# Turning three of the four branch outputs through DRAM and VectorE instead of TensorE, in a two-layer hybrid mixer

## The chip, the cores and the metric

The program runs on one core of a Trainium2 chip. The metric is the device time of one execution in microseconds. Besides the matrix engine (TensorE, PE in the profile) the core has a vector engine (DVE), a scalar engine (ACT), GpSimd (POOL, which here does hardly anything but issue DMAs) and SyncE (SP, which issues the loads of the weights).

## The reference

The reference is a decoder trunk of two layers over 256 tokens of width 2048. Cut to what is computed in a layer:

```python
xn = rmsnorm(h)
z  = xn @ w_in                      # one projection, cut into segments
o0 = forgetting_attention(q, k, v, f) * silu(gate)      # "fox"
o1 = differential_attention(q, k, v)  * silu(gate)      # "diff"
o2 = rmsnorm(ssd_chunked(conv(xbc), dt) * silu(z))      # "ssd", Mamba-2
o3 = glu(gelu(s5_scan(u))) * silu(gate)                 # "s5"
# each o_n: 256 tokens x 512
m  = sum(sigmoid(g[n]) * (o[n] @ w_branch[n]) for n in range(4))
h  = h + rmsnorm(m @ w_out)
```

All is in float32. Every `o[n] @ w_branch[n]` needs `o[n]` with its 512 channels on the partitions, since TensorE contracts over partitions, while the branches leave it with the tokens on the partitions. So each of the eight blocks of 128 tokens by 512 channels in a layer (four branches, two token blocks) has to be turned. The change is to six of them.

## The kernel before, in words

The matrix products run as one long stream on TensorE. `plan()` (L48) lists the weight matrices in order, in column groups of 512; `group` (L404) does one group: for each k-tile of 128 rows of weights and each of the two token blocks three matmuls of 128 by 512, because the float32 operands are split in a high and a low part: high weight by high activation (L423), high by low (L424), low by high (L425). The weights come in chunks of four k-tiles by one SP DMA each of 1 MB (`prefetch`, L340) into `raw`. ACT makes the high part `wh` from it, and VectorE the low part `wl` as `raw - wh`, both two k-tiles at a time (128 by 1024 elements). There are five such half-chunk buffers of each kind. L101 and L113 are helpers for two-operand VectorE work and for ACT work, and L110 is VectorE's `scalar_tensor_tensor`, so many different things show those lines and are told apart by their tiles.

Everything else (attention, the convolution, the scans) is written as Python generators, which `pump` (L379) advances between chunks, as far as a budget of costs goes. A generator that yields WAIT pauses until the next chunk. `drain` (L397) runs a generator to its end. After that a scheduler fixes the order of the instructions on each engine, and each engine works its own list in order.

The branches `fox` (L462), `diff` (L551) and `ssd` (L640) leave their outputs in tiles `fxo`, `dfo` and `xst` (two each, one for each token block) in `st["o", n, tb]`. The gates of the merge follow in `plan()` as groups mg(n, cg) of 16 k-tiles, and after the four gate groups of a branch come its four products br(n, cg) of 4 k-tiles each. In the third chunk of mg(n, 0) the hook `turn_o` drains the branch and calls `o_split` (L531): for each token block four transposes on TensorE (`split_T`, L293, the instruction at L298) through a PSUM bank `mx`, then ACT copies the high part `oh` and VectorE makes the low part `ol`. The br groups use `oh` and `ol` as stationary operands. For the fourth branch the same is done late in its gates.

The S5 branch (`s5`, L779) runs beside the gates. For each of four slices of its channels it loads a table `s5b` (L838), writes `uu` to DRAM and fetches it back in another layout (`du` L852, `s5u` L862: four fetches of 128 KB), multiplies that with `s5bs` on TensorE (L885) and scans on VectorE. All of these DMAs stand on POOL's queue, which works its list in order; a DMA that has to wait for data holds up those behind it.

A second way of turning a block is in the kernel already, for q, k and the convolution's inputs: `put` (L315) writes a block to DRAM in four pieces, `get` (L321) reads it back with four neighbouring tokens on one partition (`shuf`), and VectorE's transpose of 32 by 32 blocks (`flip_pair`, L327) finishes it. The channels then come out in another order, given by the permutation P in `_layout` (L1213), and the columns of the weights that made them are permuted to match when the inputs are laid out on the host.

Of the kernel before, what the change touches and what calls it, by code (L numbers as in the profile page):

```python
# [10 lines left out]
F32 = mybir.dt.float32  # L11
# [6 lines left out]
ADD, SUB, MUL, MAX, MIN = ALU.add, ALU.subtract, ALU.mult, ALU.max, ALU.min  # L18
# [11 lines left out]
WAIT = -1  # L30
# [39 lines left out]
def trunk(ctx: ExitStack, tc: tile.TileContext, x, xT0, wall, cst, prm, rows, lam, normg, postg, s5b, s5c, out):  # L70
# [391 lines left out]
    def fox(st):  # L462
        lf = st["sp"]
        qT = [blk("foxqT", (128, 2, 256)) for _ in range(2)]
        kT = [blk("foxkT", (128, 2, 256)) for _ in range(2)]
        Xs = [[get(d) for d in st[src]] for src in ("fq", "fk")]
        yield WAIT
        yield WAIT
        for dst, X in zip((qT, kT), Xs):
            for hp in range(2):  # L470
                flip_pair(dst[hp], X, hp)
                yield 1.25
        bm = [blk("bm", (128, 3, 128)) for _ in range(4)]
        for kb in range(2):
            ps = mx()
            for hd in range(4):
                o = ps[:, hd * 128:(hd + 1) * 128]
                PE.matmul(o, lhsT=bc(lf[:, 0, hd:hd + 1], [128, 128]), rhs=bc(one, [128, 128]) if kb else U,
                          start=True, stop=kb == 0)
                if kb:  # L480
                    PE.matmul(o, lhsT=bc(lf[:, 1, hd:hd + 1], [128, 128]), rhs=U, start=False, stop=True)
            p3 = ps.rearrange("p (h k) -> p h k", h=4)

            for hd in range(4):
                tt(bm[hd][:, 2 * kb], p3[:, hd], tri, ADD)
                if kb == 0:
                    act(bm[hd][:, 1], p3[:, hd])
            yield 0.8
        yield WAIT
        E, pt, pso = {}, {}, {}  # L490
        rs = [small([128, 4], "fx_rs") for _ in range(2)]

        def scores(i):
            qb, hd = divmod(i, 4)
            nk = (qb + 1) * 128
            ps = mx()[:, 0:nk]
            PE.matmul(ps, lhsT=qT[hd // 2][:, hd % 2, qb * 128:(qb + 1) * 128], rhs=kT[hd // 2][:, hd % 2, 0:nk],
                      start=True, stop=True)
            S = blk("S", (128, 256))
            m = small([128, 1], "fx_m", bufs=4)  # L500
            b = bm[hd][:, 0] if qb == 0 else bm[hd][:, 1:3].rearrange("p a k -> p (a k)")
            V.tensor_tensor_reduce(out=S[:, 0:nk], in0=ps, in1=b, scale=1.0, scalar=-3.0e38,
                                   op0=ADD, op1=MAX, accum_out=m)
            ts(m, m, -1.0)
            E[i] = blk("E", (128, 256))
            act(E[i][:, 0:nk], S[:, 0:nk], AF.Exp, bias=m, scale=1.0, accum_out=rs[qb][:, hd:hd + 1])
            return 0.3 + 0.13 * qb

        def turn(i):
            pt[i] = probs_T(E.pop(i), i // 4 + 1)  # L510
            return 0.0

        def values(i):
            qb, hd = divmod(i, 4)
            if hd == 0:
                pso[qb] = mx()
            pv(pso[qb], pt.pop(i), st["fv"], hd, qb + 1)
            if hd < 3:
                return 0.0
            ri = small([128, 4], "fx_ri")  # L520
            V.reciprocal(ri, rs[qb])
            o = blk("fxo")
            for hd in range(4):
                c = slice(hd * 128, (hd + 1) * 128)
                stt(o[:, c], pso[qb][:, c], ri[:, hd:hd + 1], st["fg"][qb][:, c], MUL, MUL)
            st["o", 0, qb] = o
            return 1.0

        yield from pipeline(8, (scores, turn, values), STEP)

    def o_split(st, n):  # L531
        st["oT", n] = []
        for tb in range(2):
            oh, ol = blk("oh", (128, 4, 128), F32R), blk("ol", (128, 4, 128), F32R)
            split_T(lambda i: (oh, ol), st["o", n, tb], 4)
            st["oT", n].append((oh, ol))

    def rope(src, tb):
# [12 lines left out]
    def diff(st):  # L551
        l = st["l"]

        qT = [[blk("difqT", (128, 2, 256)) for _ in range(2)] for _ in range(2)]
        kT = [blk("difkT", (128, 2, 256)) for _ in range(2)]
        halves = [cs[:, C_HALF + a:C_HALF + a + 1] for a in range(2)]
        li = 0.8 - 0.6 * math.exp(-0.3 * l)
        sub = rw[:, l, R_SUB:R_SUB + 128].unsqueeze(1).to_broadcast([128, 4, 128])
        r = {}
        for nm in ("dq", "dk"):  # L560
            for tb in range(2):
                r[nm, tb] = rope(st[nm][tb], tb)
                yield 2.0
            g3 = st["dg"][nm == "dk"].rearrange("p (h d) -> p h d", h=4)
            tt(g3, g3, sub, MUL)
            yield 0.6
        yield WAIT
        Xs = {nm: [get(r[nm, tb]) for tb in range(2)] for nm in ("dk", "dq")}
        yield WAIT
        yield WAIT  # L570
        yield WAIT
        for hp in range(2):
            flip_pair(kT[hp], Xs["dk"], hp)
            yield 1.25
        for hp in range(2):
            full = blk("difqf", (128, 2, 256))
            flip_pair(full, Xs["dq"], hp)
            for a in range(2):
                act(qT[hp][a], full, AF.Copy, scale=halves[a])
            yield 1.25  # L580
        yield WAIT
        E, pt, pso, rs = {}, {}, {}, {}

        def scores(i):
            qb, hd = divmod(i, 4)
            nk = (qb + 1) * 128
            ps = mx().rearrange("p (a k) -> p a k", a=2)
            S = blk("S2", (128, 2, 256))
            E[i] = blk("E2", (128, 2, 256))
            m = small([128, 2], "df_m", bufs=4)  # L590
            rs[i] = small([128, 2], "df_rs", bufs=6)
            for a in range(2):
                PE.matmul(ps[:, a, 0:nk], lhsT=qT[hd // 2][a][:, hd % 2, qb * 128:(qb + 1) * 128],  # L593
                          rhs=kT[hd // 2][:, hd % 2, 0:nk], start=True, stop=True)
                V.tensor_tensor_reduce(out=S[:, a, 0:nk], in0=ps[:, a, 0:nk], in1=tri if qb == 0 else mask2,
                                       scale=1.0, scalar=-3.0e38, op0=ADD, op1=MAX, accum_out=m[:, a:a + 1])
            ts(m, m, -0.125)
            for a in range(2):
                act(E[i][:, a, 0:nk], S[:, a, 0:nk], AF.Exp, bias=m[:, a:a + 1], scale=0.125,
                    accum_out=rs[i][:, a:a + 1])  # L600
            return 0.5 + 0.26 * qb

        def combine(i):
            nk = (i // 4 + 1) * 128
            e, q = E[i], rs[i]
            V.reciprocal(q, q)
            tt(q[:, 1:2], q[:, 1:2], nlam[:, l], MUL)
            ts(e[:, 0, 0:nk], e[:, 0, 0:nk], q[:, 0:1])
            stt(e[:, 0, 0:nk], e[:, 1, 0:nk], q[:, 1:2], e[:, 0, 0:nk], MUL, ADD)
            return 0.5 + 0.2 * (i // 4)  # L610

        def turn(i):
            pt[i] = probs_T(E.pop(i)[:, 0], i // 4 + 1)
            return 0.0

        def values(i):
            qb, hd = divmod(i, 4)
            if hd == 0:
                pso[qb] = mx()
            pv(pso[qb], pt.pop(i), st["dv"], hd, qb + 1)  # L620
            if hd < 3:
                return 0.0
            o, sq = blk("dfo"), blk("dfsq")
            sq3 = sq.rearrange("p (h d) -> p h d", h=4)
            ss = small([128, 4], "df_ss")
            act(o, pso[qb])
            tt(sq, o, o, MUL)
            V.tensor_reduce(out=ss, in_=sq3, axis=AX.X, op=ADD)
            rst = small([128, 4], "df_rst")
            rsqrt(rst, ss, 4, 1.0 / 128, EPS)  # L630
            ts(rst, rst, 1.0 - li)
            for hd in range(4):
                c = slice(hd * 128, (hd + 1) * 128)
                stt(o[:, c], o[:, c], rst[:, hd:hd + 1], st["dg"][qb][:, c], MUL, MUL)
            st["o", 1, qb] = o
            return 3.2

        yield from pipeline(8, (scores, combine, turn, values), STEP)

    def ssd(st):  # L640
        l = st["l"]
# [108 lines left out]
        def out_of(tb):  # L750
# [10 lines left out]
            act(junk, y, AF.Square, accum_out=ss)  # L761
            rsqrt(rst, ss, 1, 1.0 / W, EPS)
            stt(y, y, rst, ng, MUL, MUL)
            st["o", 2, tb] = y

        out_of(0)
        yield 2.8
# [7 lines left out]
        yield 1.2  # L775
        out_of(1)
        yield 2.8

    def s5(st):  # L779
        l = st["l"]  # L780
# [423 lines left out]
def _layout(i):  # L1204
# [10 lines left out]
    for l in range(L):  # L1215
        for kind, arg, ncol, nk in plan():
# [10 lines left out]
                c0 = SEG["mg"] + arg[0] * D + arg[1] * 512  # L1227
                w = w_in[l][:, c0:c0 + 512]
            elif kind == "br":
                w = w_br[l, arg[0]][:, arg[1] * 512:(arg[1] + 1) * 512]  # L1230
            elif kind == "glu":
                w = w_glu[l][:, arg * 512:(arg + 1) * 512]
            else:
# [65 lines left out]
```

## Time and profile before

| | us |
|---|---|
| median of 3 runs | 1764.84 |
| the runs | 1764.58, 1764.84, 1767.0 |
| the profiled execution | 1764.39 |
| its span in the trace | 1762.6 |
| granted TensorE clock, mean | 0.998 of full speed |

| engine | busy us | share of the span | instructions |
|---|---|---|---|
| PE | 1743.3 | 99% | 8198 |
| DVE | 1331.0 | 76% | 2403 |
| ACT | 838.5 | 48% | 1131 |
| POOL | 71.6 | 4% | 122 |

The span is what the trace covers, and 1.8 us of the profiled execution lie around it. Times in the rows below count from the start of the span. TensorE's busy time runs from the start of a matmul to its modelled end, so that neighbouring matmuls overlap; what one costs in the stream is the distance from its start to the next start. Queries of one stretch here are all of the first layer unless the text says otherwise; the second layer has the same stretches about 875 us later.

### The profile page before, as it was taken

What the parts mean: (1) busy time and instruction counts of PE and PEld (TensorE: products, weight loads), DVE (VectorE), ACT (ScalarE), POOL (GpSimd) and SP (SyncE); (2) the same over time, 40 slices, a digit from 0 to 9 for tenths busy, and PEclk for the clock granted to TensorE, in tenths of its full rate; (3) what the DMA queues carried; (4) which work ended last, traced back from release to release, by engine and by line L of the source; (5) the groups of instructions that cost most, each with busy time, mean ns of one, the idle gap of its engine ahead of it and who ended that gap; (6) DMA issues with size and microseconds to landing.
All of it is one profiled execution on the core that took longest, in us unless ns stands there. A gap on an engine that the chain in (4) does not pass through costs nothing.

```text
span 1762.6 us, 22152 instructions
## 1 busy us (share of the span) xinstructions
PE 1743.3 (99%) x8198; PEld 1444.4 (82%) x8198; DVE 1331.0 (76%) x2403; ACT 838.5 (48%) x1131; POOL 71.6 (4%) x122
## 2 busy tenths in 40 slices
PE   9999999999999999999999999999999999999997
PEld 7888888888888878888889888888888888788886
DVE  6765467997999999575674655669979999985754
ACT  7445445454444444444464454564544444444442
POOL 0000020000100000000000000100010000000000
PEclk9999999999999999999999999999999999999999
DMA  9664574355655655555555645744555655556452
GB/s 359 222 224 159 195 275 167 145 215 181 200 209 186 221 192 190 215 191 179 183 200 200 227 149 197 268 168 164 200 189 194 227 181 195 210 183 220 181 191 96
DMA packets 58893, 350.21 MB, mean 199 GB/s; under 512 B 7456, under 2 KB 11680, under 8 KB 20384
## 3 DMA queue, kind: packets, MB, share of 16 engines
q1 hardware_dynamic: 46640, 322.04, 51.1%
q0 software_dynamic: 12000, 26.75, 4.8%
q8 instruction: 64, 1.05, 0.2%
q14 instruction: 45, 0.37, 0.1%
q10 hardware_dynamic: 144, 0.01, 0.0%
HBM read 338.28 MB, written 10.49 MB: 198 GB/s over the span
## 4 chain that ended last, share of the span: by engine, by line
PE 88%; DVE 9%; issue 2%; DMA 1%; ACT 0%; POOL 0%; DVEq 0%; SPq 0%; ACTq 0%
PE acc L423 28%; PE acc L425 28%; PE acc L424 28%; DVE wl L101 2%; PE mx L298 1%; DVE Et L101 1%; DVE s5w L101 1%; DVE s5t L101 1%; PE mx L593 1%; PE mx L460 1%; DVE s5a L101 1%; DVE s5a L903 1%; DVE mt L110 1%; DMA s5u<-du 1%; DVE Etm L101 1%
## 5 line engine op out<-in xcount | busy, mean ns | idle before, releaser
L113 ACT ACTIVATE wh<-raw 128x1024 fp32r<-128x1024 f32 (+1 forms) x586 | 619.2, 1061 | 745.8 <-PE acc L424 635.2
L101 DVE TENSOR_TENSOR wl<-raw,wh 128x1024 fp32r<-128x1024 f32 (+1 forms) x586 | 713.3, 1223 | 342.4 <-ACT wh L113 327.0
L423 PE MATMUL acc<-wh,xh 128*128 128x512 f32 (+1 forms) x1896 | 730.7, 385 | 0.5 <-ACT sig L113 0.5
L425 PE MATMUL acc<-wl,xh 128*128 128x512 f32 (+1 forms) x1896 | 725.5, 384 | 3.3 <-DVE wl L101 3.3
L424 PE MATMUL acc<-wh,xl 128*128 128x512 f32 (+1 forms) x1896 | 726.0, 383 | 0.0
L425 PEld LDWEIGHTS acc<-wl,xh 128*128 128x128 f32 x1896 | 355.4, 188 | 74.8 <-DVE wl L101 5.9
L423 PEld LDWEIGHTS acc<-wh,xh 128*128 128x128 f32 x1896 | 356.1, 188 | 70.7 <-ACT sig L113 1.4
L424 PEld LDWEIGHTS acc<-wh,xl 128*128 128x128 f32 x1896 | 356.3, 188 | 66.7
L423 PE MATMUL acc<-wh,oh 128*128 128x512 f32 x256 | 100.9, 394 | 0.0
L424 PE MATMUL acc<-wh,ol 128*128 128x512 f32 x256 | 99.8, 390 | 0.0
L425 PE MATMUL acc<-wl,oh 128*128 128x512 f32 x256 | 99.7, 390 | 0.0
L423 PE MATMUL acc<-wh,mh 128*128 128x512 f32 x224 | 87.7, 391 | 0.0
L425 PE MATMUL acc<-wl,mh 128*128 128x512 f32 x224 | 87.3, 390 | 0.0
L424 PE MATMUL acc<-wh,ml 128*128 128x512 f32 x224 | 87.2, 389 | 0.0
L113 ACT ACTIVATE sig<-acc,rhalf 128x512 f32<-128x512 f32 x64 | 42.7, 683 | 31.9 <-PE acc L425 24.9
L423 PEld LDWEIGHTS acc<-wh,oh 128*128 128x128 f32 x256 | 48.1, 188 | 10.3 <-issue 0.8
L425 PEld LDWEIGHTS acc<-wl,oh 128*128 128x128 f32 x256 | 48.1, 188 | 10.2
L424 PEld LDWEIGHTS acc<-wh,ol 128*128 128x128 f32 x256 | 48.1, 188 | 9.4
L425 PEld LDWEIGHTS acc<-wl,mh 128*128 128x128 f32 x224 | 42.0, 188 | 8.8
L423 PEld LDWEIGHTS acc<-wh,mh 128*128 128x128 f32 x224 | 42.1, 188 | 8.5
L424 PEld LDWEIGHTS acc<-wh,ml 128*128 128x128 f32 x224 | 42.1, 188 | 8.4
L903 DVE TENSOR_TENSOR_SCAN s5a<-S5R,s5w 128x256 f32<-128x256 f32 x64 | 40.6, 678 | 0.0
(333 smaller groups left out, 1363.0 us busy)
## 6 DMA issues: line engine op xcount, KB each, us to landing
raw<-in_wall_dram SPq DMA_DIRECT2D x290, 1024.0 KB, 4.8
raw<-in_wall_dram SPq DMA_DIRECT2D x8, 1048.0 KB, 5.0
shuf<-d POOLq DMA_DIRECT2D x24, 256.0 KB, 6.4
s5b<-in_s5b_dram POOLq DMA_DIRECT2D x16, 256.0 KB, 3.5
s5u<-du POOLq DMA_DIRECT2D x32, 128.0 KB, 3.8
h<-in_x_dram SPq DMA_DIRECT2D x2, 1024.0 KB, 9.5
d<-ropea POOLq DMA_DIRECT2D x8, 256.0 KB, 3.0
du<-uu POOLq DMA_DIRECT2D x8, 256.0 KB, 2.3
```

The lines of the kernel that those rows point to most:

```text
L101: V.tensor_tensor(out=out, in0=a, in1=b, op=op)
L110: V.scalar_tensor_tensor(out=out, in0=a, scalar=s, in1=b, op0=op0, op1=op1)
L113: A.activation(out, a, f, **kw)
L298: PE.transpose(ps[:, i * 128:(i + 1) * 128], src[:, i * 128:(i + 1) * 128], ident)
L423: PE.matmul(o, lhsT=sh, rhs=rh, start=k == 0, stop=False)
L424: PE.matmul(o, lhsT=sl, rhs=rh, start=False, stop=False)
L425: PE.matmul(o, lhsT=sh, rhs=rl, start=False, stop=k == nk - 1)
L460: PE.matmul(pso[:, c], lhsT=pt[:, b], rhs=v[b][:, c], start=b == 0, stop=b == nb - 1)
L593: PE.matmul(ps[:, a, 0:nk], lhsT=qT[hd // 2][a][:, hd % 2, qb * 128:(qb + 1) * 128], rhs=kT[hd // 2][:, hd % 2, 0:nk], start=True, stop=True)
L903: V.tensor_tensor_scan(out=a[:, r], data0=rr, data1=w[:, r], initial=0.0, op0=MUL, op1=ADD)
```

## The change

The outputs of the first three branches are written to DRAM as soon as they are made (`put`, two 256 KB DMAs of a branch in a layer), and after a pause of at least one chunk read back shuffled (`o_get`, two more). `o_split` then turns each with one VectorE transpose of 32 by 32 blocks over 128 by 512 elements, out of SBUF into SBUF, and ACT and VectorE make the two parts from that tile instead of from PSUM. The rows of the weights of these three branches are permuted on the host, as the channels now come in the order P. The fourth branch keeps its transposes on TensorE.

```diff
@@ fox
-            st["o", 0, qb] = o
+            st["o", 0, qb] = put(o)
             return 1.0
         yield from pipeline(8, (scores, turn, values), STEP)
+        yield WAIT
+        o_get(st, 0)
+
+    def o_get(st, n):
+        for tb in range(2):
+            st["o", n, tb] = get(st["o", n, tb])

     def o_split(st, n):
         st["oT", n] = []
         for tb in range(2):
             oh, ol = blk("oh", (128, 4, 128), F32R), blk("ol", (128, 4, 128), F32R)
-            split_T(lambda i: (oh, ol), st["o", n, tb], 4)
+            if n == 3:
+                split_T(lambda i: (oh, ol), st["o", n, tb], 4)
+            else:
+                r = blk("oT", (128, 4, 128))
+                V.transpose(out=r.rearrange("p k (t i) -> p i k t", i=4),
+                            in_=st["o", n, tb].rearrange("p i (k c) -> p i k c", c=32))
+                act(oh, r)
+                tt(ol, r, oh.bitcast(F32), SUB)
             st["oT", n].append((oh, ol))
@@ diff
-            st["o", 1, qb] = o
+            st["o", 1, qb] = put(o)
...
+        yield WAIT
+        o_get(st, 1)
@@ ssd
-            st["o", 2, tb] = y
+            st["o", 2, tb] = put(y)
...
+        yield WAIT
+        o_get(st, 2)
@@ _layout
-                w = w_br[l, arg[0]][:, arg[1] * 512:(arg[1] + 1) * 512]
+                w = w_br[l, arg[0]][P if arg[0] < 3 else slice(None), arg[1] * 512:(arg[1] + 1) * 512]
```

The scheduler makes of this the following orders. On POOL, from the last shuffles of the rotary branch to the first slice of S5, the first layer before (`s5c`, `ng` and `s5b` are tables for ssd and S5):

```order
L324 DMA shuf<-d 128x512 x7
L816 DMA s5c<-in_s5c_dram 128x512 x2
L748 DMA ng<-in_normg_dram 128x512
L838 DMA s5b<-in_s5b_dram 128x512 x2
L852 DMA du<-uu 128x512
L862 DMA s5u<-du 64x2x256 x4
```

And the same place now, in which the lines of what is unchanged have moved down by the added ones:

```order
L324 DMA shuf<-d 128x512 x7
L318 DMA d<-dfo 128x4x128 x2
L324 DMA shuf<-d 128x512 x2
L833 DMA s5c<-in_s5c_dram 128x512 x2
L763 DMA ng<-in_normg_dram 128x512
L318 DMA d<-xst 128x4x128
L855 DMA s5b<-in_s5b_dram 128x512
L318 DMA d<-xst 128x4x128
L855 DMA s5b<-in_s5b_dram 128x512
L869 DMA du<-uu 128x512
L324 DMA shuf<-d 128x512 x2
L879 DMA s5u<-du 64x2x256 x4
```

The write and the read of diff's output stand ahead of the S5 table, the second `s5b` load now stands behind the second write of ssd's output, and the two reads of ssd's output stand between `du` and the four `s5u` fetches.

On VectorE at the third branch's turn, in the first layer before (`s5a`, `s5t`, `s5w`, `Et`, `Etm` belong to S5's scans):

```order
L101 TENSOR_TENSOR wl<-raw,wh 128x1024
L101 TENSOR_TENSOR s5t<-s5a,Et 128x512
L101 TENSOR_TENSOR s5w<-s5a,Et 128x512
L101 TENSOR_TENSOR wl<-raw,wh 128x1024
L101 TENSOR_TENSOR ol<-mx,oh 128x512 x2
L101 TENSOR_TENSOR s5a<-s5w,s5t 128x256 x2
L101 TENSOR_TENSOR Et<-E_2960 128x256
L101 TENSOR_TENSOR Etm<-E_2961 128x256
L101 TENSOR_TENSOR Et<-E_2960,E_2961 128x256
L101 TENSOR_TENSOR Et<-Et,Etm 128x256
L101 TENSOR_TENSOR Etm<-E_2961,E_2960 128x256
L101 TENSOR_TENSOR wl<-raw,wh 128x1024
```

And now, where directly ahead of the first row shown stand a first STREAM_TRANSPOSE of L545 and one `wl`:

```order
L101 TENSOR_TENSOR ol<-oT,oh 128x512
L545 STREAM_TRANSPOSE oT<-shuf 128x4x128
L101 TENSOR_TENSOR s5t<-s5a,Et 128x512
L101 TENSOR_TENSOR s5w<-s5a,Et 128x512
L101 TENSOR_TENSOR ol<-oT,oh 128x512
L101 TENSOR_TENSOR s5a<-s5w,s5t 128x256 x2
L101 TENSOR_TENSOR Et<-E_2972 128x256
L101 TENSOR_TENSOR Etm<-E_2973 128x256
L101 TENSOR_TENSOR Et<-E_2972,E_2973 128x256
L101 TENSOR_TENSOR Et<-Et,Etm 128x256
L101 TENSOR_TENSOR Etm<-E_2973,E_2972 128x256
L101 TENSOR_TENSOR wl<-raw,wh 128x1024
```

Before, the fourth row is the `wl` of the first half-chunk of br(2, 0), ahead of the `ol` pair. Now that half-chunk is the last row shown, behind both transposes, the `ol` and S5's work. On TensorE that group began with L423, L424, L425 of the first token block, then the same of the second; now it begins with L423, L424 of both blocks and then has the two L425. Apart from that TensorE's order is the old one without the six groups of eight transposes; the place of the third of them was this:

```order
L425 MATMUL acc<-wl,xh 128x512
L298 MATMUL mx<-cs,xst 128x128 x8
L885 MATMUL mx<-s5u,s5bs 128x256 x2
L423 MATMUL acc<-wh,xh 128x512
L424 MATMUL acc<-wh,xl 128x512
```

Now L885 follows the L425 directly. SP's order is unchanged.

## Rows read from the trace of the kernel before

**Rows 1.** The page: the chain of work that ended last, by engine.

```profile
PE 88%; DVE 9%; issue 2%; DMA 1%; ACT 0%; POOL 0%; DVEq 0%; SPq 0%; ACTq 0%
```

**Rows 2.** Waits of PE: us in total, times, longest us.

```profile
PE acc L425 <- DVE wl L101: 3.3, 6, 1.2
PE mx L885 <- DMA s5u<-du: 2.1, 2, 1.1
```

**Rows 3.** Timeline of PE at fox's turn: start us, us, engine, line, operation.

```profile
329.54 0.39 PE L425 MATMUL acc<-wl,xh 128*128 128x512 f32 x1
329.77 1.03 PE L298 MATMUL mx<-cs,fxo 128*128 128x128 f32 x8
330.56 0.48 PE L423 MATMUL acc<-wh,xh 128*128 128x512 f32 x1
330.88 0.40 PE L424 MATMUL acc<-wh,xl 128*128 128x512 f32 x1
```

**Rows 4.** DMA issues: tiles, queue, count, KB each, median us to landing.

```profile
shuf<-d POOLq DMA_DIRECT2D x24, 256.0 KB, 6.4
d<-ropea POOLq DMA_DIRECT2D x8, 256.0 KB, 3.0
```

**Rows 5.** The tile fxo: duration ns min/median/max, first and last start.

```profile
L110 DVE SCALAR_TENSOR_TENSOR fxo<-mx,fx_ri,fg x16: 341/344/354, 166.1 to 1044.8; 128x128 f32<-128x128 f32 x16
```

**Rows 6.** Timeline of POOL, first layer, 364 to 442 us.

```profile
365.12 0.54 POOL L816 DMA_DIRECT2D s5c<-in_s5c_dram  x1 [113.80 <-DVE UAl L101]
...
415.96 0.54 POOL L838 DMA_DIRECT2D s5b<-in_s5b_dram  x1 [1.18 <-DVE xst L101]
...
439.77 2.40 POOL L862 DMA_DIRECT2D s5u<-du  x4 [2.24 <-PE acc L425]
```

**Rows 7.** Timeline of DVE, four stretches of the first layer.

```profile
334.59 2.02 DVE L330 STREAM_TRANSPOSE xT<-shuf 128x256 f32<-128x256 f32 x4
336.44 1.22 DVE L101 TENSOR_TENSOR wl<-raw,wh 128x1024 fp32r<-128x1024 f32 x1
...
348.96 2.37 DVE L101 TENSOR_TENSOR wl<-raw,wh 128x1024 fp32r<-128x1024 f32 x2
...
430.10 0.75 DVE L110 SCALAR_TENSOR_TENSOR xst<-xst,sd_rst,ng 128x512 f32<-128x512 f32 x1
...
565.18 1.21 DVE L101 TENSOR_TENSOR wl<-raw,wh 128x1024 fp32r<-128x1024 f32 x1
566.29 0.69 DVE L101 TENSOR_TENSOR s5t<-s5a,Et 128x512 f32<-128x512 f32 x1
...
567.50 1.23 DVE L101 TENSOR_TENSOR wl<-raw,wh 128x1024 fp32r<-128x1024 f32 x1
568.63 1.29 DVE L101 TENSOR_TENSOR ol<-mx,oh 128x512 fp32r<-128x512 f32 x2
569.83 0.76 DVE L101 TENSOR_TENSOR s5a<-s5w,s5t 128x256 f32<-128x256 f32 x2
...
572.18 1.23 DVE L101 TENSOR_TENSOR wl<-raw,wh 128x1024 fp32r<-128x1024 f32 x1
```

**Rows 8.** Timeline of PE, first layer: two uses of wl, and ssd's turn.

```profile
353.78 0.39 PE L425 MATMUL acc<-wl,xh 128*128 128x512 f32 x1
...
565.70 1.03 PE L298 MATMUL mx<-cs,xst 128*128 128x128 f32 x8
...
572.73 0.39 PE L425 MATMUL acc<-wl,oh 128*128 128x512 f32 x1
```

**Rows 9.** Windows: us, busy PE PEld DVE ACT POOL (x), PEclk, DMA share, GB/s.

```profile
444.00:464.00 20.00, 18.99 (x91) 15.73 (x91) 16.11 (x23) 9.74 (x12) 1.15 (x2) 1.00 0.59 196
438.00:440.00 2.00, 2.00 (x11) 1.65 (x10) 1.29 (x2) 1.06 (x1) 0.23 (x1) 1.00 0.45 139
440.00:442.00 2.00, 2.00 (x10) 1.67 (x9) 2.00 (x5) 0.63 (x1) 2.00 (x4) 1.00 0.87 303
```

**Rows 10.** Timeline of ACT, first layer, at the second s5b table.

```profile
434.16 0.61 ACT L113 ACTIVATE s5bs<-s5b 128x512 fp32r<-128x512 f32 x1
```

## The prediction, made before the changed kernel was run

> **What bounds the kernel now.** I read the chain of waits first. TensorE holds 88% of it and VectorE 9% [rows 1], so time taken out of TensorE's stream counts in full where TensorE waits for nothing, and not where VectorE is late. The list of TensorE's waits says where it waits: 3.3 us in all for the low weight halves `wl`, in six places, and 2.1 us, in two places (one a layer), for the S5 data `s5u`, which come over POOL's DMA queue [rows 2]. Both are small, but both are on engines or queues to which the change adds work. So the question is not whether TensorE gets shorter; it does. It is whether VectorE and POOL's queue can carry the load at the three places in a layer where the outputs are turned.
>
> **What is removed.** In the stream of full matmuls one starts every 0.23 us (329.54 to 329.77). From the L425 at 329.54, over eight transposes, to the second matmul behind them at 330.88 is 1.34 us [rows 3]; two ordinary distances (0.46) belong to the L425 and the L423, so a group of eight costs 1.34 - 0.46 = 0.88 us of TensorE time. Six groups (three branches, two layers): -5.3 us, 0.30% of the time. The PSUM evacuations by ACT and VectorE are not removed, they only read SBUF instead; I cost that at nothing.
>
> **The detour itself.** A write lands in 3.0 us and a shuffled read in 6.4 [rows 4], so some 10 us from the output to its shuffled copy. Fox's first output is written from 166.1 [rows 5] and is turned at 329.77 [rows 3]; ssd's last one at 430.10 [rows 7] and is turned at 565.70 [rows 8]. Diff's write stands in POOL's order ahead of the S5 table's load, which was issued at 365.12 [rows 6] after 113.80 us of idle queue; diff is turned between fox and ssd, in the stretch from 444 to 464 [rows 9]. All three reads are hidden by the gate products that lie between, with a margin of tens of microseconds. What costs is not the latency but what else they push aside.
>
> **VectorE: two new transposes at each turn.** No transpose of 128x512 is in the trace. Four of 128x256 start at 334.59 and the next instruction at 336.44 [rows 7]: 0.46 us each. If a transpose went by instruction alone, the new one would take 0.46, at worst a rate below twofold would make it about 1.2, as a `wl` of 128x1024 does [rows 7]; I take twice the row, 0.92, since it is the same operation with twice the elements. That is 1.84 us of VectorE at each of six turns.
>
> At fox's turn this is hidden: the next tight weight half is the first of the pair at 348.96 (done some 1.2 us later, at about 350.1) and TensorE uses it at 353.78 [rows 7, 8], a margin of 3.6 us, of which about half would be left. At diff's turn VectorE is busy for 16.1 of 20 us [rows 9]; 3.9 us of idle time take up the 1.84. If that cover failed I would lose up to 1.84 us there.
>
> At ssd's turn it is not hidden. VectorE works without a pause from 565.18 to 573 [rows 7], S5's scans beside the weights, and the order has moved one `wl`, the first of br(2, 0), from ahead of the `ol` pair to behind everything. I add up the new order from 565.18, each instruction by the distance to the next start [rows 7]: transpose 0.92; `wl` 1.11 (565.18 to 566.29); first `ol` 0.60 (half of 568.63 to 569.83); transpose 0.92; `s5t` and `s5w` 1.21 (566.29 to 567.50); second `ol` 0.60; the `s5a` pair and five small products on `Et` 2.35 (569.83 to 572.18). Sum 7.71: that `wl` starts at 572.89 and ends 1.23 later, at 574.12. TensorE wanted it at 572.73 [rows 8]. Now it wants it 0.88 earlier for the transposes that are gone behind 565, and 0.46 later because two matmuls have been put ahead of the L425: 572.31. So TensorE stops for 1.8 us. With transposes of 0.46 it would be 0.9, with 1.2 each 2.4; if VectorE comes to 565 half a microsecond earlier or later than before, as much less or more. I take 1.8 a layer, +3.6 us in two (1.0 to 5.4).
>
> **POOL's queue: S5's first slice.** The four fetches `s5u` were issued from 439.77, after a pause of 2.24 us behind `du` [rows 6], and it is for these that TensorE waits already, at most 1.1 us [rows 2]. So a delay of `s5u` comes through undiminished. There are two sources.
>
> First, the reads of ssd's output, 512 KB, are now issued between `du` and `s5u`. Their issue (about 0.54 each) fits in the time from 437.5 to 439.8 in which the queue waited for `du` to land. Their bytes do not quite: from 438 to 440 the DMA engines are busy by 0.45 at 139 GB/s, from 440 to 442 by 0.87 at 303 GB/s, with a weight chunk [rows 9]. 512 KB at 303 GB/s are 1.7 us. About 1 us is free before 440 (2 us by 0.55), of which the reads, which can't flow before `du` has, get perhaps 0.6: so 1.1 us of delay. The bounds: 0 if the reads and the weights share so that `s5u` is served as before, since weights have slack and `s5u` hasn't; 3.8 if the reads go at no more than 139 GB/s and `s5u` waits for all of them (524 KB / 139).
>
> The Trainium skill says, in "DMA: Bandwidth & Descriptors", section "Queues, rings and completion order", that a DMA engine takes turns between queues, but consumes the descriptors of one ring in their order. By that the weights, on SP's queue, can't be put behind `s5u`, and `s5u` does wait for both reads; the sum would then have 3.8 in place of 1.1, 5.4 us more in two layers. No row here shows two kinds of transfers on POOL's queue that close together with weights beside them.
>
> Second, the second `s5b` load, issued at 415.96 before [rows 6], now stands behind the write of ssd's second output, which is made from 430.10 to 430.85 [rows 7]. A write and the load together need about 0.7 us of issue, so the load starts at about 431.6 and lands about 3 us later, at 434.6, where ACT wanted it at 434.16 [rows 10]; behind that on ACT stands the `uu` from which `du` is made. I take 0.4 (0 to 1.0).
>
> Together 1.5 us a layer, +3.0 us in two (0 to 9.6).
>
> **The sum.** -5.3 + 3.6 + 3.0 = +1.3 us against the profiled execution: 1764.39 + 1.3 = 1765.7. The median of the runs shown is 0.45 above it, so 1766.1. The span and the 1.8 us around it are not touched otherwise.
>
> **The rivals.**
>
> (A) The full gain. VectorE reaches 565 earlier by what TensorE has saved before, the scans have room, and the reads of ssd's output are served in the gap before `s5u`. Speaks for it: TensorE's waits are a few tenths of a percent in all [rows 2], and 24% of VectorE's time is free. Against it: at 565 none is free. 1764.84 - 5.3 = 1759.5.
>
> (B) Slower, by POOL's queue. `s5u` waits behind both reads at the slow rate, 3.8 us, and for the late `s5b` 0.4: 8.4 us in two layers, with 3.6 at ssd's turn: -5.3 + 12.0 = +6.7, so 1771.5. It decides from the point where stall and delay together exceed the 2.65 us that a layer saves; at 1.8 for the turn that is from 0.9 us of delay, and 0.2% are passed from 2.6 us. For it: the existing wait is TensorE's, so nothing covers it. Against: most of the time the reads have is before the weights come.
>
> The Trainium skill's page "VectorE: DVE Perf Modes" gives as a rule, in "Rules for kernel authors", that a 128x128 transpose goes to TensorE where PSUM will do as its destination. By it the change is the wrong way round, which is what (B) and (C) would show; the rows speak for it only where VectorE has no pause.
>
> (C) VectorE is the bound of the whole stretch in which it is late (3.3 us of waits, in six places [rows 2]): the turn of diff and that of ssd then cost their transposes, 1.84 a turn, and the TensorE time taken out there comes back as waits, so that only fox's 0.88 remain. 2 x (2 x 1.84 - 0.88) = +5.6, and the waits of S5 come less to bear, as they lie in the same stretch: about 1769.5.
>
> (D) The change doesn't do what it says, as TensorE's transposes were hidden. The rows exclude that: the stream's next matmul starts 0.88 late [rows 3].
>
> **How the numbers follow.** A measurement of this kernel can tell about 0.2% from no change, 3.5 us: under 1761.3 is faster, over 1768.4 slower. My forecast, both stalls at about their sizes, 0.57, with a range of its own of 1762 to 1769; (A) 0.13; (B) 0.18; (C) 0.12. Of the forecast's 0.57 some 0.05 falls under and 0.05 over the bounds, of (A) and (C) a quarter each into "same", and of (B) a sixth. That makes faster 0.15, same 0.56, slower 0.29. The range reaches from between (A) and the forecast, 1761, up to just short of (B), 1770.5.
>
> **What would show it.** In the profile after: no L298 with `fxo`, `dfo` or `xst`; VectorE's transposes of 128x512 at a distance of about 0.9; TensorE waiting for `wl` at the first L425 of br(2, 0), 1.8 us in each layer, where before it waited for nothing; TensorE's wait for `s5u` at the first slice up from about 1 to about 2.5, with the two shuffled reads landing between `du` and `s5u`. The prediction is wrong if the wait at br(2, 0) is missing (then VectorE got there earlier, and (A) is near), if the wait for `s5u` goes past 3.5 (B), or if the `wl` waits grow in places before ssd's turn (C).

## The result, and the profile after

The changed kernel takes 1778.12 us (median of 6 runs, 1775.43 to 1781.71), the kernel before 1765.09 beside it: ratio 1.0076, 95% interval 1.0065 to 1.0087. That is slower by 13 us. One of the six runs of the kernel before took 5681.35 us, and below one of e4's eleven 2176.71; the ratios leave these two out. The forecast was 1766.1, at the most 1770.5. The profiled execution took 1775.80 us (span 1773.9), the quicker end of its runs.

The waits of TensorE come first (us in total, times, longest), changed kernel:

```profile
PE mx L902 <- DMA s5u<-du: 10.9, 2, 7.8
PE acc L425 <- DVE wl L101: 6.7, 8, 1.7
PE acc L423 <- ACT sig L113: 2.9, 2, 1.6
PE acc L423 <- ACT bwh L113: 1.6, 1, 1.6
```

(`sig` is ACT's sigmoid of a gate group. ACT reads it from the buffer `acc`, into which TensorE's next group goes. The wait for `bwh` lies at the start of the program and was 1.5 before.) Against [rows 2] the wait for `s5u` has grown by 8.8 us, that for `wl` by 3.4, in two more places. The wait for `sig` is 2.9 where the same view of before had 0.5. Together +14.6; less the 5.3 us of transposes that is +9.3 of the 11.3 us by which the span grew. What the granted clock adds is below.

TensorE at the first S5 slice of the first layer (start, us, engine, line, operation, idle before and releaser):

```profile
443.01 0.39 PE L425 MATMUL acc<-wl,xh 128*128 128x512 f32 x1
451.23 0.77 PE L902 MATMUL mx<-s5u,s5bs 128*128 128x256 f32 x2 [7.83 <-DMA s5u<-du]
451.79 0.63 PE L423 MATMUL acc<-wh,xh 128*128 128x512 f32 x1
452.22 0.63 PE L424 MATMUL acc<-wh,xl 128*128 128x512 f32 x1
...
453.93 0.58 PE L425 MATMUL acc<-wl,xh 128*128 128x512 f32 x1
454.34 0.40 PE L423 MATMUL acc<-wh,xh 128*128 128x512 f32 x1
454.58 0.40 PE L424 MATMUL acc<-wh,xl 128*128 128x512 f32 x1
```

The wait is 7.83 us, and behind it a matmul starts every 0.43 us instead of every 0.23 [rows 3], for six of them: 1.2 us more. The windows show why, by the granted clock, which is the third number from the end (columns as in [rows 9]):

```profile
440.00:443.00 3.00, 3.00 (x14) 2.46 (x14) 3.00 (x5) 2.79 (x4) 1.60 (x3) 1.00 0.34 101
451.20:454.30 3.10, 3.07 (x8) 2.58 (x9) 1.34 (x2) 0.00 (x0) 0.46 (x1) 0.50 0.88 355
454.30:457.00 2.70, 2.70 (x13) 2.17 (x12) 0.00 (x0) 1.23 (x2) 0.00 (x0) 1.00 0.16 65
```

After the wait TensorE works at the lower of its two levels, 1.2 instead of 2.4 GHz, and then at the full one again. In the second layer the wait is 3.0 us and the clock stays at 1.00. The other runs show a lower clock: the six have a mean granted clock of 0.997, 0.992, 0.995, 0.994, 0.993 and 0.995, beside 0.997 to 0.999 of the kernel before; the two slowest, at 1781.21 and 1781.71, are those with 0.992 and 0.993.

Why `s5u` came late, on POOL's queue:

```profile
430.33 0.77 POOL L318 DMA_DIRECT2D d<-xst  x1 [9.11 <-DVE xst L110]
431.09 0.54 POOL L855 DMA_DIRECT2D s5b<-in_s5b_dram  x1
440.68 0.54 POOL L869 DMA_DIRECT2D du<-uu  x1 [9.05 <-DVE uu L101]
441.21 1.07 POOL L324 DMA_DIRECT2D shuf<-d  x2
443.47 2.42 POOL L879 DMA_DIRECT2D s5u<-du  x4 [1.19 <-DMA du<-uu]
```

and on ACT, which needs the second `s5b` for `s5bs` and makes `uu` only behind that:

```profile
438.57 0.63 ACT L113 ACTIVATE s5bs<-s5b 128x512 fp32r<-128x512 f32 x1 [5.14 <-DMA s5b<-in_s5b_dram]
439.11 0.36 ACT L113 ACTIVATE uu<-mx 128x256 fp32r<-128x256 f32 x1
```

The second `s5b` load was issued at 431.09, as forecast (431.6), but was in ACT's hands only at 438.57, 7.5 us later, where I had counted 3. So `s5bs` moved back by 4.4 us against [rows 10] and the issue of `s5u`, behind `uu` and `du`, by 3.7 against [rows 6], and `s5u` took longer to arrive besides: from the issue at 443.47 to L902 at 451.23 are 7.8 us; before it were 5.5 (439.77 [rows 6] to 445.23):

```profile
445.23 0.47 PE L885 MATMUL mx<-s5u,s5bs 128*128 128x256 f32 x2 [1.01 <-DMA s5u<-du]
```

That is the row of the kernel before. In the second layer of the changed kernel the load landed 3.0 us after its issue and ACT waited 0.6 us for it, so that it was mostly the second part of this that happened, hence 3.0 us instead of 7.8.

VectorE at ssd's turn, to be read against [rows 7], and the use of the `wl` on TensorE:

```profile
572.87 1.05 DVE L545 STREAM_TRANSPOSE oT<-shuf 128x512 f32<-128x512 f32 x1
573.77 1.20 DVE L101 TENSOR_TENSOR wl<-raw,wh 128x1024 fp32r<-128x1024 f32 x1
...
575.49 1.08 DVE L545 STREAM_TRANSPOSE oT<-shuf 128x512 f32<-128x512 f32 x1
576.41 0.68 DVE L101 TENSOR_TENSOR s5t<-s5a,Et 128x512 f32<-128x512 f32 x1
...
580.53 1.22 DVE L101 TENSOR_TENSOR wl<-raw,wh 128x1024 fp32r<-128x1024 f32 x1
```

```profile
579.75 0.39 PE L424 MATMUL acc<-wh,ol 128*128 128x512 f32 x1
581.80 0.73 PE L425 MATMUL acc<-wl,oh 128*128 128x512 f32 x2 [1.67 <-DVE wl L101]
```

Here the forecast holds: a transpose costs 0.90 to 0.92 us (572.87 to 573.77, 575.49 to 576.41), the last `wl` of the rows starts 7.66 us after the first of them (7.71 forecast), and TensorE stops for 1.67 (1.8).

### The profile page after: what moved, and what is told of

It reads as the page before. It is cut to its first block, busy times and chain, and to the rows that moved or that the text cites. A ratio compares the mean times of both kernels' runs of the same rounds, so it can differ in the third digit from the quotient of the medians.

```text
span 1773.9 us, 22119 instructions
## 1 busy us (share of the span) xinstructions
PE 1740.1 (98%) x8150; PEld 1440.5 (81%) x8150; DVE 1340.0 (76%) x2415; ACT 839.4 (47%) x1131; POOL 87.3 (5%) x146
## 4 chain that ended last, share of the span: by engine, by line
PE 85%; DVE 11%; issue 3%; DMA 1%; ACT 0%; POOL 0%; DVEq 0%; SPq 0%; ACTq 0%; POOLq 0%
PE acc L425 27%; PE acc L423 27%; PE acc L424 27%; DVE wl L101 3%; DVE s5w L101 1%; DVE Et L101 1%; DVE s5t L101 1%; DVE s5a L101 1%; DVE s5a L920 1%; DMA s5u<-du 1%; PE mx L298 1%; PE mx L606 1%; DVE Etm L101 1%; PE mx L460 1%; DVE mt L110 1%
## 5 line engine op out<-in xcount | busy, mean ns | idle before, releaser
L423 PE MATMUL acc<-wh,xh 128*128 128x512 f32 (+1 forms) x1896 | 730.8, 386 | 2.9 <-ACT sig L113 2.9
L425 PE MATMUL acc<-wl,xh 128*128 128x512 f32 (+1 forms) x1896 | 726.0, 384 | 3.4 <-DVE wl L101 3.4
L424 PE MATMUL acc<-wh,xl 128*128 128x512 f32 (+1 forms) x1896 | 726.5, 383 | 0.0
L425 PEld LDWEIGHTS acc<-wl,xh 128*128 128x128 f32 x1896 | 355.7, 188 | 74.8 <-DVE wl L101 5.9
L423 PEld LDWEIGHTS acc<-wh,xh 128*128 128x128 f32 x1896 | 356.6, 188 | 73.4 <-ACT sig L113 3.8
L424 PEld LDWEIGHTS acc<-wh,xl 128*128 128x128 f32 x1896 | 356.6, 188 | 66.8
L425 PE MATMUL acc<-wl,oh 128*128 128x512 f32 x256 | 99.7, 391 | 3.4 <-DVE wl L101 3.4
L423 PE MATMUL acc<-wh,oh 128*128 128x512 f32 x256 | 100.8, 394 | 0.0
L424 PE MATMUL acc<-wh,ol 128*128 128x512 f32 x256 | 99.8, 390 | 0.0
L423 PE MATMUL acc<-wh,mh 128*128 128x512 f32 x224 | 87.7, 391 | 0.0
L425 PE MATMUL acc<-wl,mh 128*128 128x512 f32 x224 | 87.3, 390 | 0.0
L424 PE MATMUL acc<-wh,ml 128*128 128x512 f32 x224 | 87.3, 390 | 0.0
L425 PEld LDWEIGHTS acc<-wl,oh 128*128 128x128 f32 x256 | 47.9, 188 | 14.2 <-DVE wl L101 4.2
L423 PEld LDWEIGHTS acc<-wh,oh 128*128 128x128 f32 x256 | 48.1, 188 | 10.4 <-issue 0.8
L424 PEld LDWEIGHTS acc<-wh,ol 128*128 128x128 f32 x256 | 48.1, 188 | 9.4
L425 PEld LDWEIGHTS acc<-wl,mh 128*128 128x128 f32 x224 | 42.1, 188 | 8.7
L423 PEld LDWEIGHTS acc<-wh,mh 128*128 128x128 f32 x224 | 42.1, 188 | 8.6
L424 PEld LDWEIGHTS acc<-wh,ml 128*128 128x128 f32 x224 | 42.1, 188 | 8.5
```

The source lines that it names most:

```text
L423: PE.matmul(o, lhsT=sh, rhs=rh, start=k == 0, stop=False)
L424: PE.matmul(o, lhsT=sl, rhs=rh, start=False, stop=False)
L425: PE.matmul(o, lhsT=sh, rhs=rl, start=False, stop=k == nk - 1)
```

## The experiments

Theories: **Q1**, the late `s5b` load makes most of the loss; **Q2**, the reads of ssd's output between `du` and `s5u` do; **V**, VectorE's transposes do and the queue is incidental. For e5, e6 and e8 **O**, what VectorE costs is a matter of order, against **L**, of its load. For e9 **G**, diff's gain is given back at the wait for `sig`, against **H**, every branch off TensorE is worth its 1.8 us.

| run | us | ratio to before (95%) |
|---|---|---|
| changed kernel | 1778.12 | 1.0076 (1.0065 to 1.0087) |
| e1, `s5b` first | 1774.95 | 1.0057 (1.0043 to 1.0071) |
| e2, reads late | 1772.34 | 1.0042 (1.0029 to 1.0055) |
| e3, both | 1766.70 | 1.0009 (1.0001 to 1.0018) |
| e4, ssd on TensorE | 1762.55 | 0.9989 (0.9980 to 0.9998) |
| e5, e3 with ssd's turn earlier | 1764.83 | 1.0002 (0.9993 to 1.0011) |
| e6, e4 with diff's turn earlier | 1762.66 | 0.9985 (0.9976 to 0.9993) |
| e7, before with two reads | 1772.93 | 1.0045 (1.0032 to 1.0058) |
| e8, all mended | 1763.90 | 0.9993 (0.9984 to 1.0002) |
| e9, fox alone | 1764.31 | 1.0002 (0.9992 to 1.0011) |

**e1, the s5b loads ahead of the writes.** The writes wait in the program until `s5b` is issued, and the reads follow without a pause:

```diff
-            st["o", 2, tb] = put(y)
+            st["o", 2, tb] = y
...
         yield 2.8
-        yield WAIT
+        for _ in range(1):
+            yield WAIT
...
+        with tc.issue_after(st["s5b"].ins):
+            for tb in range(2):
+                st["o", 2, tb] = put(st["o", 2, tb])
         o_get(st, 2)
```

> The changed kernel with one thing undone on POOL's queue: both s5b loads of the first S5 slice stand ahead of the writes of ssd's output again; the reads of that output still stand between du and s5u. In the trace of the changed kernel TensorE waits 10.9 us for s5u (7.8 in the first layer, 3.1 in the second) where it waited 2.1. Theory Q1 (the late s5b load delays uu and du, and that is most of it): uu comes back by about 4 us in the first layer, the wait falls to 1 to 2 us a layer, and the time to about 1767 to 1768. Theory Q2 (the two reads ahead of s5u are most of it, as they push s5u into the next weight chunk): the wait stays at 3 us or more a layer and the time at 1771 or above. Theory V (the loss is VectorE's, the queue is incidental): no change, 1776 to 1778.

1774.95: above Q1's number, in Q2's. `uu` is in time again (`du` is issued at 436.01), and TensorE still waits 3.0 us in the first layer and 3.3 in the second. And what stands behind the wait weighs as much as it:

```profile
PE mx L907 <- DMA s5u<-du: 6.3, 2, 3.3
PE acc L423 <- ACT sig L113: 3.7, 2, 1.9
PE acc L425 <- DVE wl L101: 3.6, 8, 1.1
```

```profile
1325.90:1331.00 5.10, 5.10 (x14) 3.94 (x13) 1.49 (x2) 0.23 (x1) 0.30 (x1) 0.50 0.60 239
```

The granted clock is at half for all of the 5.1 us behind the second layer's wait. In the windows of this run it also falls behind the first layer's and behind both waits for `sig`: 40 matmuls start at the half clock, each 0.20 us later than at the full one, some 8 us in all. The wait for `wl` at br(2, 0) is gone in this run (3.6 in all, 3.3 before), though VectorE's order there is that of the changed kernel; TensorE came to it later, held up at the half clock behind the wait for `sig`.

**e2, the reads behind s5u.** One pause becomes four, so that the reads come after the fetches:

```diff
         yield 2.8
-        yield WAIT
+        for _ in range(4):
+            yield WAIT
         o_get(st, 2)
```

> The changed kernel with the other thing undone: the reads of ssd's output stand behind the four s5u fetches of the first slice; the second s5b load still stands behind the second write. Q1: the wait for s5b stays (ACT waits up to 5 us for it), TensorE's wait for s5u stays at 3 us or more in at least one layer, the time at 1771 or above. Q2: the wait for s5u falls to 1 to 2 us a layer, the time to about 1767. V: no change, 1776 to 1778.

1772.34: Q1's number this time. ACT waits for `s5b` as in the changed kernel, and TensorE for `s5u` in the first layer:

```profile
438.10 0.63 ACT L113 ACTIVATE s5bs<-s5b 128x512 fp32r<-128x512 f32 x1 [5.23 <-DMA s5b<-in_s5b_dram]
```

```profile
448.87 0.76 PE L903 MATMUL mx<-s5u,s5bs 128*128 128x256 f32 x2 [6.04 <-DMA s5u<-du]
```

**e3, both.** The diff of e1 with a `yield WAIT` ahead of `o_get`.

> Both undone: s5b ahead of the writes, the reads behind s5u; nothing else of the change is touched, so all transposes stay on VectorE. Q1 and Q2 alike: TensorE's wait for s5u is back at about 1 us a layer; left are the 5.3 us saved on TensorE, 3.9 us of waits for wl at br(2, 0) and 2.5 us of more waiting for sig behind br(1, 0) to br(1, 3): -5.3 + 3.9 + 2.5 = +1.1, about 1766. V: still above 1772.

1766.70, as expected, with the waits expected (2.5 for `s5u`, 6.8 for `wl`, 3.0 for `sig`). V falls. Added to e3, the reads cost 8.2 us (e1 less e3) and the late `s5b` 5.6 (e2 less e3). Together they cost 11.4 and not 13.8. The waits themselves do add up: in the first layer they are longer than before by 1.95 us in e1, 5.03 in e2 and 6.82 in the changed kernel. In the profiled runs the clock does not: 40 matmuls start at the half clock in e1, 12 in e2 and 8 in the changed kernel. So a time of one of these kernels is in part a matter of where the clock fell.

**e4, ssd back on TensorE.**

```diff
-            if n == 3:
+            if n >= 2:
                 split_T(lambda i: (oh, ol), st["o", n, tb], 4)
...
-                w = w_br[l, arg[0]][P if arg[0] < 3 else slice(None), arg[1] * 512:(arg[1] + 1) * 512]
+                w = w_br[l, arg[0]][P if arg[0] < 2 else slice(None), arg[1] * 512:(arg[1] + 1) * 512]
```

> The third branch goes back to TensorE's transposes (rows of its weights not permuted); fox and diff keep the detour. If the whole loss sits with the third branch (Q1, Q2, and the wait for wl at br(2, 0)), the wait for s5u is 2 us again, that at br(2, 0) is gone, and the time is 4 x 0.88 = 3.5 us under before less what VectorE gives back for diff (the wait for sig, up to 2.5): 1761.6 to 1764. If a detour costs wherever it stands (V), two thirds of the loss remain: about 1773.

The write and the read of ssd's output are left out with it. 1762.55, in the expected range: the whole loss sat with the third branch, and fox and diff alone are a small gain (2.2 us, its interval just clear of none).

**e7, the suspected cost alone, in the kernel before.** Two loads of a table that nothing uses, between `du` and `s5u`:

```diff
         def prep_b(pc):
+            if pc == 0:
+                for _ in range(2):
+                    nc.gpsimd.dma_start(out=blk("xtra"), in_=s5c[l, 0])
```

> The kernel before with one suspected cost alone: two more loads of 256 KB (a table, whose copies nothing uses) between du and s5u of the first slice in each layer; no transpose is changed. Theory Q2 with the clock: s5u lands about 2 us later in each layer, TensorE waits 3 us for it instead of 1, and the granted clock is at half for the 2 to 4 us behind the wait, which costs another 1 to 2.5 us a layer: +6 to +9, 1771 to 1774. Q2 without the clock: +4, 1769. If the reads in that place cost nothing without the late s5b and VectorE's transposes: 1764 to 1766.

1772.93, 8.15 above its before: as Q2 with the clock expects, and the 8.2 us by which e1 and e3 differ. With nothing changed on TensorE or VectorE, half a megabyte at this place costs this much:

```profile
PE mx L888 <- DMA s5u<-du: 7.0, 2, 4.4
```

```profile
448.20:452.20 4.00, 4.00 (x11) 3.23 (x12) 0.00 (x0) 0.00 (x0) 0.00 (x0) 0.50 0.56 217
```

4.9 us are waits (7.0 less 2.1), and the half clock behind them makes about 4 more. From L888, at 448.15, to the fourteenth start behind it are 5.47 us, and in the kernel before, from its L885 at 445.23, 3.06:

```profile
453.62 0.39 PE L423 MATMUL acc<-wh,xh 128*128 128x512 f32 x1
```

```profile
448.29 0.39 PE L423 MATMUL acc<-wh,xh 128*128 128x512 f32 x1
```

That is 2.4 us in the first layer; the same fourteen starts take 1.6 us longer in the second.

**e5, e3 with ssd turned one chunk earlier.**

```diff
-                group(xstat, nk, ncol, ev, hook={2: turn_o} if cg == (3 if n == 3 else 0) else None)
+                group(xstat, nk, ncol, ev, hook={(1 if n == 2 else 2): turn_o} if cg == (3 if n == 3 else 0) else None)
```

> The kernel with both queue orders undone (e3_both, 1766.7 us, 1.9 above before), in which the third branch is turned one chunk earlier (second chunk of its first gate group, some 5.4 us), so that the first wl of br(2, 0) no longer stands behind both transposes. Theory O (the 1.98 us that TensorE waits there in each layer comes from the order, VectorE as a whole has room): that wait goes, nothing else comes, 1766.7 - 3.9 = 1762.8. Rival L (VectorE's load decides, the two transposes cost their time wherever they stand in this stretch): the wait turns up at another wl nearby, 1765.5 to 1767.

1764.83, between the two. The wait at br(2, 0) is gone (`wl` waits 3.7 in all, 3.3 before), as O says. But the wait for `sig` grew from 3.0 to 3.9 us, and behind it the clock fell in this run, in both layers, as it had not in e3:

```profile
549.90:553.40 3.50, 3.50 (x10) 2.76 (x9) 3.47 (x7) 0.89 (x2) 0.00 (x0) 0.52 0.88 300
```

So this profile does not show O by itself, for in e1, where the clock fell at the same place, that wait is gone with the order unchanged. e8 does, below. The profiled run, at 1766.53, is also the slowest of e5's eleven.

**e6, e4 with diff turned two chunks earlier** (the same edit with 0 for n == 1).

> The kernel with the third branch on TensorE (e4_ssd_on_PE, 1762.55 us), in which diff's output is turned two chunks earlier, before the first S5 slice arrives. In e4_ssd_on_PE the 0.88 us saved at diff's turn is given back behind br(1, 0) to br(1, 3): TensorE waits there for sig, sig for the end of a table product on VectorE. Theory O: the transposes now stand where VectorE is idle, the scans start and end earlier against TensorE, the wait for sig returns to about 0.5 us, and the time falls by 1 to 1.5, to about 1761.3. Rival L (VectorE is behind by its own chain from the arrival of s5u on, whatever stands before it): no change, 1762.5.

1762.66: no change, L's number. The wait for `sig` did shrink (2.0 to 1.3 us), so neither theory is clean; the difference is below what these runs tell apart.

**e8, e3 with both turns earlier** (0 for diff, 1 for ssd).

> All mended together: the detour for three branches, s5b ahead of the writes, the reads behind s5u, diff turned two chunks and ssd one chunk earlier. Theory O: the full gain of six groups, less a few tenths: 1764.8 - 5.3 = 1759.5 to 1760.5. Rival L: at least one of the waits on VectorE comes back, 1762 to 1766.

1763.90, L's range, and not distinguishable from before. Here the clock stays at 1.00 from the wait for `sig` past br(2, 0), and TensorE does not wait for `wl` in this stretch, so that the order is what removes the wait at br(2, 0):

```profile
545.00:617.00 72.00, 70.69 (x328) 57.56 (x326) 70.25 (x120) 33.55 (x40) 4.10 (x7) 1.00 0.57 195
```

But TensorE now waits for `oT`, `sig` and `wl` in other places (2.4, 2.7 and 4.5 us; the first stands where it waited 2.1 for `s5u`): the gain is 5.3 us, and VectorE gives most of it back in small pieces.

**e9, fox alone.**

> Only the first branch takes the detour; diff and ssd are turned on TensorE as before. Its two groups of eight transposes save 2 x 0.88 = 1.8 us and its turn lies ahead of the stretch in which VectorE is late. Theory G (diff's gain is given back at the wait for sig, so fox alone is worth as much as fox and diff together): 1763.0, and TensorE's wait for sig is back at 0.5 us. Rival H (every branch off TensorE is worth its 1.8 us, and fox and diff together measured 2.2 for other reasons): the two together stay clearly ahead of fox alone, which would be at 1763.5 or above with sig waiting as long as with both.

1764.31, no change, with TensorE waiting 1.9 us for `sig`: G falls, and H's numbers are met (though the intervals of e4 and e9 overlap). H's premise is not: fox alone should be worth 1.8 us by it, and is worth nothing that these runs can tell. Most of it goes back at the wait for `sig`, which was 0.5. That wait is therefore not made by diff's transposes. VectorE in e9, then in the kernel before, shows where it starts:

```profile
538.55 0.76 DVE L101 TENSOR_TENSOR s5w<-s5a,s5t 128x256 f32<-128x256 f32 x2 [2.21 <-DMA du<-uu]
```

```profile
537.81 0.76 DVE L101 TENSOR_TENSOR s5w<-s5a,s5t 128x256 f32<-128x256 f32 x2 [0.84 <-DMA du<-uu]
```

VectorE's scan waits for the end of the last slice's `du` write, which `s5w` does not read; presumably, and not shown, it takes over the buffer of `uu`. All the scans, the table products and `sig` behind them move by that. In every kernel with the detour this wait is longer (1.9 to 4.5 us in all, 3.6 in the changed kernel; 1.2 before and in e7). Why the same write ends later there I have not found.

The version that beats both kernels is e4 or e6, at 0.11 to 0.15% under before.

## Why the prediction was wrong

**The gain** was right: the six groups are gone, and TensorE's stream moves forward by 0.79 to 0.89 us at each, against the same matmuls of before.

**The detour's latency** was right as far as it went: no turn waits for its shuffled copy.

**VectorE at ssd's turn** was right in mechanism and size: 1.67 us of waiting forecast as 1.8, from a transpose of 0.9 forecast as 0.92. e8 shows that it was the order that made it. e1 shows a condition that the forecast did not name: where TensorE itself comes late, the same order costs nothing.

**POOL's queue** is the step that failed, above all its term for the late `s5b`; it was the right place with the wrong price. I had put 1.5 us a layer; it was 6.8 and 1.9 of added waiting (7.8 and 3.0 less the 1.0 and 1.1 of before), and the clock on top. The 8.8 us lie inside the 0 to 9.6 of that term, but the bounds of the sum's own terms reach to 1774.5 (1764.84 - 5.3 + 5.4 + 9.6), and I had cut the range at 1770.5. Each term was too small, in its own way:

- "The late `s5b`: 0.4 (0 to 1.0)". I took the landing time of a load that starts into a quiet queue. Here the load started behind the write and beside a weight chunk and took 7.5 us in the first layer of both kernels that have this order (changed kernel, e2), about 3 in the second. The changed kernel issued `s5u` at 443.47, and e1, where this load is in time, at 438.82, so that the term was 4.7 in the first layer; in the second it was about the 0.6 that ACT waited. It is the term that was furthest off. A bound of 1.0 from the usual landing was no bound. All but a few packets of the first layer's load had gone by 434, 3 us after its issue; the last few went one by one between those of a weight chunk, which landed late as well (7.8 us after its issue, where the one before it took 4.7). What held them I could not tell.
- "The reads: 1.1 (0 to 3.8)". Inside the range, but too small: the waits of 3.0 and 3.3 us in e1, 4.4 and 2.6 in e7 are 1.5 to 3.4 longer than before; in the changed kernel `s5u` took 2.3 and 1.4 us longer from its issue to L902. My sum let the reads use free DMA time ahead of the weights and counted only what was over. But they held up the weight chunk too: it landed 7.3 us after its issue in e1 (438.07 to 445.38), where it took 5.1 before (439.05 to 444.12), and `s5u`, which came in with the end of that chunk before, still did: its first fetch landed at 445.67 in e1 and 444.62 before, issued 0.95 earlier.
- The granted clock was no term at all. In e7 it makes about 4 of the 8.5 us between the profiled runs. The kernel before waits 1.1 us at the same place, and its clock stays at 1.00 behind it; I had no row of before that showed a longer wait in the middle of the stream, and did not ask what one would do.

**Rival (B)** was the right one, to its place, with a time of 1771.5 that was still 7 us short. Its mechanism, `s5u` delayed by both reads, is what e1 and e7 show, though not by the reads' own transfer: in e1 they had landed at 439.69 and 440.32, and `s5u` only from 445.67 on, with the weight chunk. The Trainium skill's rule that I set beside it ("DMA: Bandwidth & Descriptors", "Queues, rings and completion order") is that one ring is worked in order and that an engine takes turns between queues. The order of landing in e1 agrees with it. Its sum, 5.4 us more, would have been nearer to the time, but by luck: for the reads it put 3.8, and they cost 1.5 to 3.4, while what was missing lay in the late `s5b`, the clock and `sig`.

**Rival (C)**, VectorE as the bound of the stretch, holds in its result and not in its sign: e8, with the queue trouble gone, is only 0.9 us under before, where the transposes make 5.3; but the waits for `wl` did not grow ahead of ssd's turn, and e9 has the wait for `sig` with fox's transposes alone. **Rival (A)** needs more than an order: no version reached 1759.5.

**The wait for `sig`** (+2.4 us) I did not foresee. It is a chain of a DMA write, a scan and a table product that ACT waits for, and e9 has it without any of the new transposes in that stretch.

## What to carry to other kernels

A queue that works in order prices what is put on it by what stands behind, not by its own length. Before moving half a megabyte onto one, look for the transfer behind it that something waits for already, and count what the addition does to the transfers of other queues that it shares the engines with. Where the matrix engine is the bound, price a new wait at its length plus what the clock may take afterwards (in e7 nearly as much again), and put a transfer's worst landing, not its median, where the margin was 18 us and is now 2 (the second `s5b`, from its issue to the moment that ACT is free for it).

## What the runs showed of the hardware that was not expected

TensorE worked at its lower level, half the clock, for 3.1 to 6.1 us behind waits of 1.9 us (for `sig`, e5), 3.0 and 3.3 (e1), 4.4 (e7) and 7.8 (the changed kernel), and a matmul then started every 0.43 us instead of every 0.23. Behind the 1.1 us of the kernel before, the 1.6 in e3, the 1.9 in e9 and the 3.0 in the second layer of the changed kernel it stayed at the full one, so the length of the wait alone doesn't decide it in these runs. And a load of 256 KB landed in about 3 us in one layer and in 7.5 in the other, with the same neighbours on its queue, in two kernels alike.
